# A three-block model on one core: weight-stream buffers paired into the experts' ring, three expert tiles moved ahead in the load order

## The chip, the core and the metric

The kernel runs on one core of one Trainium2 chip. The metric is the time of one execution on the device, in microseconds (us), as a median over runs. The core has five engines that matter here: TensorE (PE, matmuls; PEld is its weight load), VectorE (DVE), ScalarE (ACT), GpSimd (POOL) and SyncE (SP), which here does hardly anything but issue loads. Sixteen DMA engines move the data of all queues.

## The reference, cut to what matters

Three transformer-like blocks run one after another on 256 tokens of width 1024, all in fp32. The first has two layers (a state-space mixer, then attention, each with a SwiGLU feed-forward network, FFN, of width 2816). The second has a mixer (RWKV-7 and stick-breaking attention) whose output goes through the output weights w_out_2 (1024 x 1024), and a mixture of 32 experts, of which each token takes 4:

```python
top_logit, top_idx = lax.top_k(logits, TOP_K)
hid = xb @ w1[e] + b1[e]                    # 1024 -> 2048
glu = jnp.minimum(hid[:, :D_FF_EXPERT], SWIGLU_LIMIT)
lin = jnp.clip(hid[:, D_FF_EXPERT:], -SWIGLU_LIMIT, SWIGLU_LIMIT)
act = glu * jax.nn.sigmoid(SWIGLU_ALPHA * glu) * (lin + 1.0)
return (act @ w2[e] + b2[e]) * gate[:, None]  # 1024 -> 1024
```

One expert has 8 MB of w1 and 4 MB of w2; all 32 together have some 400 MB, read once. The third block is attention of two kinds and an output projection.

## The kernel before, in words

**Weights come through two readers.** Class `Stream` brings the weights of the blocks; class `Experts` brings those of the experts. Both issue their loads on SP's queue, in program order, and a load that must wait for its buffer holds up all SP loads behind it.

**The stream.** `weight_plan` writes the order of the loads by hand; `pieces` cuts each entry into pieces of at most 8 KB per partition (1 MB), most entries into two. The pool "w" has eight buffers of 8 KB per partition. `Stream.load` (L286) issues the next piece while there is room; a new piece takes the buffer that was given back first, whichever piece had it. `_split` (L299) turns one unit of a piece (two units to a piece, as a rule) into a high part on ScalarE (`wh`, L309) and a low part on VectorE or GpSimd (`wl`, L313); after the last unit of a piece `_retire` (L277) gives its buffer back. `ahead` keeps the splits three units ahead of the matmuls (two in the mixer), into four buffers (three in the mixer). `dense_F` takes three matmuls per product from these parts (helper line L514) and calls a background step (`tick`) after each unit. In the two FFNs the plan puts pieces named `ada_t` between the gate and up weights; `cond` (L1219, its operation L1225) reduces each with two VectorE operations in background steps and only then gives the buffer back.

**The second block's mixer** ends with `dense_F("w_out_2", ...)` (L1505): the first four of eight units multiply the attention half, the second four the output of `group_norm` (L1815), which runs in the background beside the first four and must be drained before the fifth. The 4 MB of w_out_2 are loaded in four pieces, as soon as w_in_2 frees buffers.

**The experts.** `moe` (L1905) opens a pool "ring" of nine buffers of 16 KB per partition, in the memory that the stream, the x pool and the mixer had (places 0 to 3 where the stream's 64 KB were, 4 and 5 over the x pool, 5 to 8 over the mixer's buffers), and loads as many of the 192 tiles of 2 MB as the ring takes, in the order of places in `RING`. A load waits for the last user of its place. An expert takes four tiles of w1 (`first`, L1994; 16 matmuls each) and two of w2 (`second`, L2043; 16 matmuls each); the order is w1 of expert 0, then w1 of e+1 and w2 of e in turn. `take` gives the tile before back and loads the next into its place. Ahead of the first expert the routing is computed, the largest count is read into registers, and `tc.If(n > 64)` (L1986 and L1987) branches over code for overfull experts, on every engine. With these inputs that code is jumped over.

After the experts the third block makes a new `Stream` with eight buffers.

Of the kernel before, what the change touches and what calls it, by code (L numbers as in the profile page):

```python
# [22 lines left out]
F32 = mybir.dt.float32  # L23
# [27 lines left out]
_n = 0  # L51
# [6 lines left out]
_n = 0  # L58
# [81 lines left out]

RING = [0, 1, 6, 7, 8, 2, 3, 5, 4]


EXPERTS = [(1, 0)] + [x for e in range(31) for x in ((1, e + 1), (2, e))] + [(2, 31)]
# [3 lines left out]
def weight_plan(stages):  # L150

    P = []
    G = []
    if "mod" in stages:
        P0 = [("ada_p", 0, 8, c * 512, 512, False) for c in range(4)]
        G = [("ada_t", r * 512, 4, 0, 1024, False) for r in range(14)]

    def fill(n):
        if "mod" in stages:
            P.extend(P0.pop(0) for _ in range(n))  # L160

    def mods(n):
        for _ in range(n):
            if G:
                P.append(G.pop(0))

    def cols(name, c0, n, nk=8, r0=0):
        P.append((name, r0, nk, c0, n, True))

    def rows4(name, total_k, ncol=1024, extra=iter(())):  # L170
        k = 0
        while k < total_k:
            n = min(4, total_k - k)
            P.append((name, k * 128, n, 0, ncol, True))
            mods(next(extra, 0))
            k += n

    def ffn(i):
        fill(2)
        at = iter(MODS[i])  # L180
        for q in range(6):
            n = 512 if q < 5 else 256
            for name in ("gate", "up"):
                cols(f"w_ffn_{name}{i}", q * 512, n)
                mods(next(at))
        rows4(f"w_ffn_down{i}", NQ, extra=at)
        P.append((f"w_ple{i}", 0, 2, 0, 1024, False))
        cols(f"w_ple_gate{i}", 0, 512)
        cols(f"w_ple_gate{i}", 512, 512)

    if "ssd" in stages:
        cols("w_in_mix", 2560, 16)
        for k, n in ((0, 2), (2, 2), (4, 4)):
            cols("w_in_mix", 2048, 512, n, k * 128)
        for c0 in (1024, 1536, 0, 512):
            cols("w_in_mix", c0, 512)
        for h in range(2):
            for b in (3600, 4624, 2576):
                cols("w_in_mix", b + 512 * h, 512)
        P.append(("w_out_mix", 1024, 4, 0, 1024, True))  # L200
        P.append(("w_out_mix", 1536, 4, 0, 1024, True))
        P.append(("w_out_mix", 0, 4, 0, 1024, True))
        P.append(("w_out_mix", 512, 4, 0, 1024, True))
        ffn(0)
    if "att" in stages:
        for c0 in (1024, 0, 512):
            cols("w_qkv", c0, 512)
        rows4("w_o", 8)
        ffn(1)
    assert not G  # L210
    if "mix" in stages:
        P.append("end")
        cols("w_in_2", 1536, 256)
        P.append(("lora", 0, 1, 0, 1024, False))
        for c0 in (512, 0, 1024, 1792, 2304, 2816):
            cols("w_in_2", c0, 512)
        P.append("end")
        rows4("w_out_2", 8)
        P.append("end")
    if "third" in stages:  # L220
        cols("w_in_3", 928, 512)
        cols("w_in_3", 1440, 512)
        cols("w_in_3", 0, 416)
        P.append(("w_uq", 0, 2, 0, 768, False))
        P.append(("w_ukv", 0, 1, 0, 1024, False))
        for c0 in (2464, 1952, 416, 4000, 4512, 2976, 3488):
            cols("w_in_3", c0, 512)
        P.append(("w_o_moba", 0, 4, 0, 1024, True))
        P.append(("w_o_mla", 0, 4, 0, 1024, True))
        cols("w_out_3", 0, 512)  # L230
        cols("w_out_3", 512, 512)
    return [c for e in P for c in ([e] if e == "end" else pieces(*e))]


def places():

    at, n = {}, 0
    for e in weight_plan(ALL):
        if e != "end" and e not in at:
            at[e] = n  # L240
            n += 128 * e[2] * e[4]
    return at


def pieces(name, r0, nk, c0, n, split):

    h = min(nk, 2048 // n)
    return [(name, r0 + k * 128, min(h, nk - k), c0, n, split) for k in range(0, nk, h)]


class Stream:


    def __init__(self, kb, plan, ring=8):
        self.kb, self.ring = kb, ring
        self.plan = []
        self.units = []
        self.fence = []
        unit = 1024
        for e in plan:  # L260
            if e == "end":
                self.fence.append(len(self.units))
                continue
            i = len(self.plan)
            self.plan.append(e)
            name, r0, nk, c0, n, split = e
            h = nk if not split else max(1, unit // n)
            for k in range(0, nk, h):
                self.units.append((i, k, min(h, nk - k), k + h >= nk, split))
        self.raws = {}  # L270
        self.splits = {}
        self.nsplit = self.used = 0
        self.pending = None
        self.room, self.nload = ring, 0
        self.depth = 3

    def _retire(self, i):  # L277
        self.room += 1
        self.load()

    def finish(self):
# [4 lines left out]
    def load(self):  # L286

        kb = self.kb
        while self.room and self.nload < len(self.plan):
            i = self.nload  # L290
            self.nload += 1
            self.room -= 1
            name, _, nk, _, n, split = self.plan[i]
            t = kb.wpool.tile([128, nk, n], F32, name=f"w_{name}_{i}", tag="w")
            o = kb.places[self.plan[i]]
            kb.nc.sync.dma_start(t.rearrange("p k n -> p (k n)"), kb.A["tiles"][o:o + 128 * nk * n].rearrange("(p m) -> p m", p=128))
            self.raws[i] = t
# [53 lines left out]
        return self.raws[i], lambda: self._retire(i)  # L351


class Experts:


    def __init__(self, kb, pool):
        self.kb, self.pool = kb, pool
        self.plan = [("exp_w1", e * 4 + k) if i == 1 else ("exp_w2", e * 2 + k) for i, e in EXPERTS for k in range(4 if i == 1 else 2)]
        self.buffers = [self.buffer(i) for i in range(len(RING))]  # L360
        self.free = list(RING)
        self.tiles, self.nload, self.used = {}, 0, 0

    def buffer(self, i):
        self._n = getattr(self, "_n", 0) + 1
        return self.pool.tile([128, 4096], F32, name=f"expert_{self._n}", tag=f"e{i}")

    def load(self):
        while self.free and self.nload < len(self.plan):
            i = self.free.pop(0)  # L370
            t, self.buffers[i] = self.buffers[i] or self.buffer(i), None
            name, r = self.plan[self.nload]
            src = self.kb.A[name][r * 128:r * 128 + 128]
            parts = 4 if self.nload == len(self.plan) - 1 else 1
            for c in range(0, 4096, 4096 // parts):
                self.kb.nc.sync.dma_start(t[:, c:c + 4096 // parts], src[:, c:c + 4096 // parts])
            self.tiles[self.nload] = i, t
            self.nload += 1
# [10 lines left out]
class KB:  # L389
# [2083 lines left out]
    def run(self):  # L2473
        nc, tc = self.nc, self.tc
        with ExitStack() as es:
            self.cpool = es.enter_context(self.pool("const", 1))
            self.fpool = es.enter_context(self.pool("residual", 1))
            outer = es
            es = outer.enter_context(ExitStack())
            self.wpool = es.enter_context(self.pool("w", 8))  # L2480
            self.xpool = es.enter_context(self.pool("x", 1))
            hes = ExitStack()
            self.hpool = hes.enter_context(self.pool("wsplit", 4))
# [7 lines left out]
                return _tl(pool, shape, dt, tag, bufs)  # L2491

            self.tl = tl
            self.st = Stream(self, weight_plan([n for n in self.stages if n != "third"]))
            xf = self.tl(self.fpool, [128, 8, T], F32, "xf")
            for k in (0, 4):
                nc.sync.dma_start(xf[:, k:k + 4], self.A["xT"][k * 128:k * 128 + 512].rearrange("(k p) n -> p k n", p=128))
# [30 lines left out]
            if "moe" in self.stages:  # L2528
                xf, stat = self.moe(xf, stat)
                self.dbg("xe", xf)  # L2530
            es = outer.enter_context(ExitStack())
            if "third" in self.stages:
                if "moe" not in self.stages:
                    with self.pool("ropetmp", 1) as C:
                        self.rope_tables(C)

                self.xpool = es.enter_context(self.pool("x", 1))
                self.wpool = es.enter_context(self.pool("w", 8))
                tpool = es.enter_context(self.pool("third", 1))
                self.st = Stream(self, weight_plan(["third"]))  # L2540
                self.st.load()
                self.third(xf, stat, tpool)
            else:
                nc.sync.dma_start(self.out.rearrange("(k p) n -> p k n", p=128), xf)
# [17 lines left out]
```

## Time and profile before

| | |
|---|---|
| median of 3 runs | 2274.73 us (2270.26 to 2278.99) |
| the profiled execution | 2268.43 us, its span 2266.6 us |
| PE, PEld busy | 94%, 66% of the span |
| DVE, ACT, POOL busy | 47%, 32%, 12% |
| moved by DMA | 618 MB, 273 GB/s on the mean |

A profile is one execution. Times in it count from the span's start. "Busy" is a share of the span; matmuls are pipelined, so that a PE in flight all the time need not be at its limit. In a row, `[4.37 <-PEq L1987]` means that the engine was idle for 4.37 us ahead of it, and what ended that. L514 is the helper that records nearly all matmuls; tiles tell them apart (acc<-expert,xe is the first expert product, py<-expert,aT the second).

### The profile page before, as it was taken

To read this page: it belongs to the slowest core of one execution; us is meant where nothing else is said; L and a number is where in the kernel's file an instruction comes from. 1 tells how busy PE (TensorE), PEld (TensorE's weight loads), DVE (VectorE), ACT (ScalarE), POOL (GpSimd) and SP (SyncE) were. 2 spreads that over 40 slices of the span, in tenths; PEclk is the share of its full clock that TensorE was granted. 3 is DMA by queue.
4 is the path that set the end of the run, shared out by engine and by line. 5 is a ranking of instruction groups with operands and counts; after the bars stand their busy time and mean duration, and the time that the engine had idled before them with its cause. 6 is when DMAs were issued, how large, how long until landed. Compare 5 with 4: busy or idle time off the path is not lost. (4 is left out here: it accounts for less than half of the span.)

```text
span 2266.6 us, 31625 instructions
## 1 busy us (share of the span) xinstructions
PE 2134.0 (94%) x13242; PEld 1500.3 (66%) x13242; DVE 1069.2 (47%) x2016; ACT 724.3 (32%) x1169; POOL 262.0 (12%) x141
## 2 busy tenths in 40 slices
PE   7999999999999988898899999999999999999997
PEld 7998998886998887788344444334333333368886
DVE  6775676566677667845122222322211212145665
ACT  5434543554544453343011110111111111133552
POOL 2332232000232002310000000000000000003101
PEclk9999999999999989898899999999999999999999
DMA  8434767432777531004999999999999999984320
GB/s 312 149 118 178 276 263 286 158 148 111 264 286 297 191 130 57 1 1 170 395 428 427 428 422 428 428 428 428 427 427 428 427 428 427 429 335 157 123 75 19
DMA packets 62098, 618.04 MB, mean 273 GB/s; under 512 B 7648, under 2 KB 10720, under 8 KB 12672
## 3 DMA queue, kind: packets, MB, share of 16 engines
q1 hardware_dynamic: 58768, 612.33, 66.8%
q10 hardware_dynamic: 3184, 3.65, 0.5%
q8 instruction: 106, 1.74, 0.3%
q14 instruction: 40, 0.33, 0.0%
HBM read 614.90 MB, written 1.05 MB: 272 GB/s over the span
## 5 line engine op out<-in xcount | busy, mean ns | idle before, releaser
L514 PE MATMUL acc<-xh,wh 128*128 128x256 f32 (+1 forms) x1736 | 494.5, 289 | 18.0 <-ACT wh L309 14.8
L514 PE MATMUL acc<-xl,wh 128*128 128x256 f32 (+1 forms) x1736 | 488.2, 285 | 1.1 <-DVE xl L553 0.3
L514 PE MATMUL acc<-expert,xe 128*64 128x512 f32 x2048 | 460.8, 600 | 28.0 <-DMA expert<-exp_w 23.5
L514 PE MATMUL acc<-xh,wl 128*128 128x256 f32 (+2 forms) x1704 | 483.4, 284 | 3.3 <-DVE wl L313 3.3
L514 PEld LDWEIGHTS acc<-expert,xe 128*64 128x64 f32 x2048 | 145.2, 138 | 313.2 <-issue 289.2
L514 PEld LDWEIGHTS acc<-xh,wh 128*128 128x128 f32 (+1 forms) x1736 | 328.2, 190 | 26.3 <-ACT wh L309 15.0
L514 PEld LDWEIGHTS acc<-xl,wh 128*128 128x128 f32 (+1 forms) x1736 | 329.5, 191 | 4.7 <-issue 1.4
L514 PEld LDWEIGHTS acc<-xh,wl 128*128 128x128 f32 (+2 forms) x1704 | 324.3, 190 | 5.6 <-DVE wl L313 4.7
L514 PE MATMUL py<-expert,aT 128*64 128x512 f32 x1024 | 234.4, 599 | 4.7 <-DMA expert<-exp_w 3.9
L2013 ACT ACTIVATE s<-a 128x512 f32<-128x512 f32 x32 | 20.2, 630 | 547.5 <-DVE a L2012 547.5
L2012 DVE TENSOR_SCALAR a<-acc 128x512 f32<-128x512 f32 x32 | 22.1, 691 | 360.3 <-PE acc L514 336.7
L2073 DVE SCALAR_TENSOR_TENSOR xf<-py,mod,xf 128x256 f32<-128x256 f32 x128 | 55.6, 479 | 283.9 <-PE py L514 283.9
L514 PEld LDWEIGHTS py<-expert,aT 128*64 128x64 f32 x1024 | 72.3, 138 | 138.3 <-issue 126.2
L313 POOL TENSOR_TENSOR wl<-w_w_in,wh 128x1024 fp32r<-128x1024 f32 (+1 forms) x11 | 26.7, 2428 | 1069.5 <-ACT wh L309 1049.6
L1225 DVE SCALAR_TENSOR_TENSOR w_ada_t<-w_ada_t,pe 128x1024 f32<-128x1024 f32 x56 | 93.3, 1688 | 0.0
L313 DVE TENSOR_TENSOR wl<-w_w_in,wh 128x1024 fp32r<-128x1024 f32 (+1 forms) x55 | 68.2, 1248 | 38.7 <-ACT wh L309 38.5
L309 ACT ACTIVATE wh<-w_w_in 128x1024 fp32r<-128x1024 f32 (+1 forms) x66 | 68.2, 1044 | 35.2 <-PE acc L514 35.1
L2060 ACT ACTIVATE y<-py 64x512 f32<-64x512 f32 x64 | 37.8, 591 | 119.2 <-PE py L514 118.6
L514 PE MATMUL tp<-sel,xh 128*128 128x128 f32 x512 | 64.3, 287 | 7.9 <-ACT aT L2040 6.9
L514 PE MATMUL acc<-wh,hh 128*128 128x512 f32 x176 | 68.7, 390 | 0.0
L514 PE MATMUL acc<-wh,hl 128*128 128x512 f32 x176 | 68.5, 389 | 0.0
L514 PE MATMUL acc<-wl,hh 128*128 128x512 f32 x176 | 68.5, 389 | 0.0
(657 smaller groups left out, 3307.9 us busy)
## 6 DMA issues: line engine op xcount, KB each, us to landing
expert<-exp_w SPq DMA_DIRECT2D x191, 2048.0 KB, 36.6
w_w_in<-tiles SPq DMA_DIRECT2D x31, 1024.0 KB, 4.9
w_ada_t<-tiles SPq DMA_DIRECT2D x28, 1024.0 KB, 6.4
w_w_ffn_gate<-tiles SPq DMA_DIRECT2D x22, 1024.0 KB, 5.0
w_w_ffn_up<-tiles SPq DMA_DIRECT2D x22, 1024.0 KB, 6.5
w_w_ffn_down<-tiles SPq DMA_DIRECT2D x22, 1024.0 KB, 6.4
w_w_in_mix<-tiles SPq DMA_DIRECT2D x21, 1024.0 KB, 8.6
w_w_out_mix<-tiles SPq DMA_DIRECT2D x8, 1024.0 KB, 4.8
```

The source lines that it names most:

```text
L309: kb.nc.scalar.activation(hi, w, AF.Copy)
L313: (kb.nc.gpsimd if far else kb.nc.vector).tensor_sub(lo, w, hi.bitcast(F32))
L514: self.nc.tensor.matmul(out, lhsT, rhs, start=start, stop=True, skip_group_check=True)
L1225: self.nc.vector.scalar_tensor_tensor(w[:, j], w[:, j], 1.0, crow[:, int(m >= 48)], op0=OP.mult, op1=OP.mult, accum_out=dst)
L2012: nc.vector.tensor_scalar(a, pg, 7.0, None, op0=OP.min)
L2013: nc.scalar.activation(s, a, AF.Sigmoid, scale=1.702)
L2060: nc.scalar.activation(y[r, o], py[r], AF.Copy)
L2073: nc.vector.scalar_tensor_tensor(xf[:, k], ps[o][:, c], gate2(k), xf[:, k], op0=OP.mult, op1=OP.add)
```

## The change

- The plan puts three entries ("early", k) between the two halves of w_out_2.
- The first `Stream` works in pairs: four buffers of 16 KB per partition (tags w0 to w3), each holding two pieces. Pairs are taken in the fixed order 3, 2, 1, 0; a new pair is begun only when both pieces that were in it are given back. The third block's stream stays as it was.
- An early entry takes a whole pair and loads an expert tile into it; that pair is never given back to the stream. The second half of w_out_2 thus comes into the pair of the first half.
- The pool "w" is opened first and stays open to the end of `moe`; its four pairs are places 0 to 3 of the ring, and the pool "ring" has places 4 to 8 alone. The three early tiles lie in places 2, 1 and 0. `RING`, the order of the other first loads, becomes 8, 7, 6, 3, 5, 4.

```diff
-RING = [0, 1, 6, 7, 8, 2, 3, 5, 4]
+RING = [8, 7, 6, 3, 5, 4]
+EARLY = 3
...
-        rows4("w_out_2", 8)
+        rows4("w_out_2", 4)
+        P.extend(("early", k) for k in range(EARLY))
+        P.append(("w_out_2", 512, 4, 0, 1024, True))
...
+    def buffer(self, p):
+        self._n = getattr(self, "_n", 0) + 1
+        return self.kb.wpool.tile([128, 4096], F32, name=f"w{p}_{self._n}", tag=f"w{p}")
+
     def _retire(self, i):
         self.room += 1
+        if self.busy:
+            self.busy[self.pair[i]] -= 1
         self.load()
...
         while self.room and self.nload < len(self.plan):
             i = self.nload
+            if self.busy:
+                early = self.plan[i][0] == "early"
+                if early and self.half % 2:
+                    self.half += 1
+                p = 3 - self.half // 2 % 4
+                if self.half % 2 == 0:
+                    if self.busy[p]:
+                        return
+                    t = self.fresh.pop(p, None)
+                    self.both = self.buffer(p) if t is None else t
+                self.busy[p] += 1
+                self.pair[i] = p
+                if early:
+                    name, r = experts_plan()[self.plan[i][1]]
+                    kb.nc.sync.dma_start(self.both, kb.A[name][r * 128:r * 128 + 128])
+                    self.early.append((p, self.both))
+                    self.half += 2
+                    self.nload += 1
+                    continue
+                self.half += 1
             self.nload += 1
             self.room -= 1
             name, _, nk, _, n, split = self.plan[i]
-            t = kb.wpool.tile([128, nk, n], F32, name=f"w_{name}_{i}", tag="w")
+            if self.busy:
+                o = (self.half - 1) % 2 * 2048
+                t = self.both[:, o:o + nk * n].rearrange("p (k n) -> p k n", n=n)
+            else:
+                t = kb.wpool.tile([128, nk, n], F32, name=f"w_{name}_{i}", tag="w")
...
-        self.buffers = [self.buffer(i) for i in range(len(RING))]
+        self.buffers = {i: self.buffer(i) for i in range(4, 9)}
         self.free = list(RING)
-        self.tiles, self.nload, self.used = {}, 0, 0
+        self.tiles = dict(enumerate(kb.st.early))
+        self.nload, self.used = len(self.tiles), 0
...
-            self.wpool = es.enter_context(self.pool("w", 8))
+            wes = outer.enter_context(ExitStack())
+            self.wpool = wes.enter_context(self.pool("w", 1))
...
-            self.st = Stream(self, weight_plan([n for n in self.stages if n != "third"]))
+            self.st = Stream(self, weight_plan([n for n in self.stages if n != "third"]), pairs=True)
...
                 xf, stat = self.moe(xf, stat)
                 self.dbg("xe", xf)
+            wes.close()
```

## Rows read from the trace of the kernel before

**Rows 1.** The page, part 2: GB/s in 40 equal slices of the span (56.7 us each).

```profile
GB/s 312 149 118 178 276 263 286 158 148 111 264 286 297 191 130 57 1 1 170 395 428 427 428 422 428 428 428 428 427 427 428 427 428 427 429 335 157 123 75 19
```

**Rows 2.** Stretches: length, busy time (instructions) of each engine, PEclk, DMA share, GB/s.

```profile
900.00:1040.00 140.00, 125.27 (x896) 110.25 (x895) 89.20 (x220) 51.31 (x90) 32.24 (x17) 0.94 0.01 2
...
1120.00:1400.00 280.00, 275.73 (x1340) 113.35 (x1337) 60.59 (x135) 34.61 (x66) 0.00 (x0) 0.99 1.01 427
```

**Rows 3.** Timeline of SP around the first expert loads: start, duration, what.

```profile
1052.79 1.28 SPq L376 DMA_DIRECT2D expert<-exp_w  x3
...
1060.77 0.33 SPq L376 DMA_DIRECT2D expert<-exp_w  x1
...
1101.59 0.34 SPq L376 DMA_DIRECT2D expert<-exp_w  x1
```

**Rows 4.** Instructions of L1987, the branch: ns min/median/max, first and last start.

```profile
L1987 SPq EVENT_SEMAPHORE  x8: 17/17/17, 1100.9 to 1101.5; - x8
...
L1987 PEldq COMPARE_BRANCH  x1: 6573/6573/6573, 1073.6 to 1073.6; - x1
```

**Rows 5.** Waits from 1060 to 1110: who for whom, total us, times, longest.

```profile
DVE a L2012 <- SPq L1987: 23.6, 1, 23.6
```

**Rows 6.** Timeline of PE over the first experts, merged.

```profile
1080.53 16.29 PE L514 MATMUL acc<-expert,xe 128*64 128x512 f32 x64 [4.37 <-PEq L1987]
...
1104.60 1.29 PE L2030 MATMUL tp<-ident,sg 128*128 128x128 f32 x4 [6.07 <-DVE sg L2025]
1105.82 15.60 PE L514 MATMUL acc<-expert,xe 128*64 128x512 f32 x64
...
1132.15 3.65 PE L514 MATMUL py<-expert,aT 128*64 128x512 f32 x16
1135.63 13.90 PE L514 MATMUL acc<-expert,xe 128*64 128x512 f32 x64
...
1190.20 13.90 PE L514 MATMUL acc<-expert,xe 128*64 128x512 f32 x64
```

**Rows 7.** Waits of PE from 1600 to 2010: total us, times, longest.

```profile
PE acc L514 <- DMA expert<-exp_w: 21.1, 21, 1.2
PE py L514 <- DMA expert<-exp_w: 3.9, 9, 0.8
```

**Rows 8.** Issue to landing: expert (1050 to 1085), w_out_2, ada_t.

```profile
DMA to landing us min/median/max: 7.9/26.5/40.1
...
DMA to landing us min/median/max: 4.8/4.8/4.8
...
DMA to landing us min/median/max: 4.7/6.4/9.1
```

**Rows 9.** Around w_out_2: SP, ACT and DVE timelines; w_in_2's last splits.

```profile
861.02 6.57 SPq L296 DMA_DIRECT2D w_w_out<-tiles  x2
...
L313 DVE TENSOR_TENSOR wl<-w_w_in,wh x11: 1210/1216/2909, 858.1 to 902.3; 128x1024 fp32r<-128x1024 f32 x11
...
1035.77 1.06 ACT L309 ACTIVATE wh<-w_w_out 128x1024 fp32r<-128x1024 f32 x1 [0.45 <-ACT wh L309]
...
1035.36 2.57 DVE L313 TENSOR_TENSOR wl<-w_w_out,wh 128x1024 fp32r<-128x1024 f32 x1 [1.65 <-ACT wh L309]
...
1040.34 0.69 DVE L1561 COPY f<-r8y 128x1024 f32<-128x1024 f32 x1
...
1042.45 0.42 DVE L1832 TENSOR_TENSOR b<-b,tp 128x256 f32<-128x256 f32 x1 [0.28 <-PE tp L1568]
```

**Rows 10.** Timelines of SP, ACT and DVE at one FFN gate of layer one.

```profile
254.57 0.33 SPq L296 DMA_DIRECT2D w_w_ffn_gate<-tiles  x1
...
272.06 1.07 ACT L309 ACTIVATE wh<-w_w_ffn_gate 128x1024 fp32r<-128x1024 f32 x1 [1.17 <-PE acc L514]
...
277.79 1.06 ACT L309 ACTIVATE wh<-w_w_ffn_gate 128x1024 fp32r<-128x1024 f32 x1 [1.83 <-PE acc L514]
...
271.35 1.21 DVE L1225 SCALAR_TENSOR_TENSOR w_ada_t<-w_ada_t,pe 128x1024 f32<-128x1024 f32 x1
```

More of the change, by code (lines that the diff above doesn't have):

```diff
@@ L231, in weight_plan @@
         cols("w_out_3", 512, 512)
-    return [c for e in P for c in ([e] if e == "end" else pieces(*e))]
+    return [c for e in P for c in ([e] if e == "end" or e[0] == "early" else pieces(*e))]
 def places():
@@ L238, in places @@
     for e in weight_plan(ALL):
-        if e != "end" and e not in at:
+        if e != "end" and e[0] != "early" and e not in at:
             at[e] = n
@@ L251, with __init__ @@
 class Stream:
-    def __init__(self, kb, plan, ring=8):
+    def __init__(self, kb, plan, ring=8, pairs=False):
         self.kb, self.ring = kb, ring
+        self.busy, self.half, self.pair, self.early = ([0] * 4 if pairs else None), 0, {}, []
+        self.fresh = {p: self.buffer(p) for p in range(4)} if pairs else {}
         self.plan = []
@@ L265, in __init__ @@
             self.plan.append(e)
+            if e[0] == "early":
+                continue
             name, r0, nk, c0, n, split = e
@@ L290, in load @@
             i = self.nload
+            if self.busy:
[16 more added lines that the diff above has]
+                    self.nload += 1
+                    continue
+                self.half += 1
             self.nload += 1
@@ L351, in hold, with experts_plan @@
         return self.raws[i], lambda: self._retire(i)
+def experts_plan():
+    return [("exp_w1", e * 4 + k) if i == 1 else ("exp_w2", e * 2 + k) for i, e in EXPERTS for k in range(4 if i == 1 else 2)]
 class Experts:
@@ L358, in __init__ @@
         self.kb, self.pool = kb, pool
-        self.plan = [("exp_w1", e * 4 + k) if i == 1 else ("exp_w2", e * 2 + k) for i, e in EXPERTS for k in range(4 if i == 1 else 2)]
-        self.buffers = [self.buffer(i) for i in range(len(RING))]
+        self.plan = experts_plan()
+        self.buffers = {i: self.buffer(i) for i in range(4, 9)}
         self.free = list(RING)
-        self.tiles, self.nload, self.used = {}, 0, 0
+        self.tiles = dict(enumerate(kb.st.early))
+        self.nload, self.used = len(self.tiles), 0
     def buffer(self, i):
         self._n = getattr(self, "_n", 0) + 1
-        return self.pool.tile([128, 4096], F32, name=f"expert_{self._n}", tag=f"e{i}")
+        pool, tag = (self.kb.wpool, "w") if i < 4 else (self.pool, "e")
+        return pool.tile([128, 4096], F32, name=f"expert_{self._n}", tag=f"{tag}{i}")
     def load(self):
@@ L370, in load @@
             i = self.free.pop(0)
-            t, self.buffers[i] = self.buffers[i] or self.buffer(i), None
+            t = self.buffers.pop(i, None)
+            t = self.buffer(i) if t is None else t
             name, r = self.plan[self.nload]
```

## The prediction

> **What bounds the kernel now.** I read the page's traffic first, then stretches around the expert stage, SP's own issue times, the matmul order, the waits, and last the places where the stream's buffers change hands. The traffic row [rows 1] shows slices 19 to 34 at about 427 GB/s. The stretches [rows 2] put the core's DMA share at 1.01 from 1120 us on, and at 0.01 from 900 to 1040: the stage that loads the experts is bound by DMA, and the 140 us ahead of it leave DMA unused. That PE looks full there too (275.73 of 280 us) does not make it the bound: two experts, 12 tiles, take 1190.20 - 1135.63 = 54.57 us of matmul order [rows 6], while DMA needs 12 x 4.9 = 58.8 us (2 MB at 427 GB/s). PE lives on the nine-tile backlog until about 1600 and then waits for tiles, 21.1 + 3.9 = 25.0 us in all [rows 7]. So an earlier end of DMA is worth its full amount up to about 25 us.
>
> The opening of the stage is where DMA loses time. SP issues the first tiles at 1052.79, the ninth at 1060.77, the tenth only at 1101.59 [rows 3]. Between them SP sits in the `If` of L1986/L1987: its eight semaphore instructions start at 1100.9 [rows 4], and the ninth load, issued at 1060.77, lands 40.1 us later [rows 8], at 1100.9. So SP leaves the `If` when all nine loads have landed, though tile 0 had been used up long before. VectorE waits for the same thing: a L2012 for 23.6 us [rows 5], of which PE feels only the end, inside the 6.07 us ahead of 1104.60 [rows 6]. With nothing queued the tenth load needs 7.9 us to land (the shortest in rows 8): 1109.5. From there DMA does not stop: 182 more loads x 4.9 = 891.8 us, last landing about 2001.
>
> **The three early tiles.** Three 2 MB loads move from 1052.79 into the idle stretch. Each waits on a pair: the first on the pair whose buffers serve the last w_out_2 loads today, 861 to 868 [rows 9], the others on the last w_in_2 splits, which start up to 902.3 [rows 9]. They cost three issues of 0.33 us on SP, which has nothing else to do there. With six tiles left, the ones in places 8, 7 and 6 of the ring are free once the group norm's last buffer there is read (f L1561, 1040.34 + 0.69 = 1041.0 [rows 9]); place 3 needs the last split, 5 and 4 the last matmuls. Six loads of 4.9 us from about 1045 land by about 1075, before the branch is reached or soon after. So SP's stall is gone.
>
> But the ring is then full and DMA idles until PE gives back tile 0. PE's first run is 16.29 us for four tiles; three at 13.90/4 = 3.47 leave 5.9 for the first [rows 6], so tile 0 is free at 1086.4, and the tenth load lands at 1086.4 + 0.1 + 7.9 = 1094.4: 15.1 us earlier than now. The 14th load needs tile 4: 1105.82 less some 2.6 us (PE was done at 1104.60 - 6.07 = 1098.5, VectorE was let go between 1100.9 and 1101.5), plus 15.60 - 3 x 3.47 = 5.2, is 1108.4, landing at 1116.4 against 1094.4 + 4 x 4.9 = 1114.0, so 2.4 lost; the 19th needs tile 9 (1132.15 + 3.65 - 2.6) and loses some 0.3. After that PE frees 12 tiles per 54.57 us, faster than DMA fills them. **Gain here: 15.1 - 2.7 = 12.4 us**, less every us by which PE starts later than 1080.53. It is not 3 x 4.9 because of the nine tiles, and it comes from the waiting `If` as much as from the early bytes.
>
> **The second half of w_out_2.** Three of four pairs now hold expert tiles, so this half can only be loaded into the pair of the first half, after its last split. That is the VectorE subtraction 1035.36 + 2.57 = 1037.9 [rows 9]; landing 4.8 us later [rows 8] is 1042.8. Today ScalarE starts the fifth unit's split at 1035.77, at once. Behind it wait, in order: on VectorE that unit's subtraction (1.2), then the group norm's multiplications, which begin at 1042.45 today. They would begin at 1042.8 + 1.1 + 0.1 + 1.2 = 1045.2, and PE's second half needs their result. **Cost 2.7 us**; bounds 0 (if VectorE's chain has that slack) and 5.1 (if the two loads share DMA and the first lands only with the second, 2.4 later). I take the worked value, since rows 8 has this very load. The fourth piece, landing 2.4 after, is split later still and costs nothing.
>
> **PE's branch.** PE's own jump at L1987 takes 6.573 us [rows 4], and PE is idle for 4.37 of it [rows 6]. It falls where expert loads have DMA full. After the change DMA has drained by then. The trace holds no jump of PE on an idle DMA, so the gain is between nothing and 4.37; I take 2.0, the middle, neither end being nearer. The Trainium skill ("Runtime: NRT & Kernel Launch", Instruction fetch mechanics) says that a taken branch outside the fetched pages must first fetch its page by DMA; no run here yet shows whether an idle DMA shortens it. By that rule the 2.0 would be nearer to 4.37 and the sum 2 us better.
>
> **The pairs.** Before, each load takes whichever of eight buffers came free first: 254.57 for a gate piece, when an older gate piece was split [rows 10]. After, pairs go round in fixed order, and in the two FFNs a pair of gate pieces follows, four pairs later, on a pair of ada_t pieces that VectorE holds for long. The gate load then waits for the last ada_t operation: 271.35 + 1.21 = 272.6, 18 us later than today. It lands at 277.4, where its first split starts at 272.06 today. PE needs that unit three units on: the split two units later starts at 277.79, one unit of PE is (277.79 - 272.06)/2 = 2.9, so 280.7. Split after landing: 277.4 + 1.06 + 0.1 + 1.21 = 279.8. **It is hidden, but by 0.9 us only.** The cover is the depth of three split units. Worked for all eight such places (four per FFN, the same rhythm), the margins are 0.35 to 1.7 us. ScalarE and VectorE stand still for 5 us each time and must catch up. I take 2 us for all eight; bounds 0 (every margin holds) and 11.5 (each load lands as late as a second one in its pair, 2.4 more, and the margins are overrun). If landing is 6.4 us, as the median of ada_t in rows 8, the cost is 5. The lora piece holds its pair as well, but the loads behind it serve splits that run on to 902.3, and today SP has issued this whole stream by 868 [rows 9]: taken as hidden. Startup, attention and the third block keep their order: DMA is far from full there [rows 1], and the third's first loads wait for the last expert tiles either way. Costed at nothing, covered by lead times of some 5 us and more beyond landing.
>
> **Sum.** 12.4 - 2.7 + 2.0 - 2.0 = 9.7 us. The profiled execution took 2268.4, so 2258.7 by it. The median of the runs shown is 6.3 higher; against 2274.7 it is **2265 us**, 0.43% less. A difference of 0.5%, 11.4 us, is about what a measurement of this kernel can tell from no change.
>
> **Rivals.**
> (a) PE's branch gives back nearly all its 4.37 us and the FFN cost is nil: 2274.7 - (12.4 - 2.7 + 4 - 0) = about 2261. For it: DMA is drained at the branch; margins are positive in all eight places. Against: a fetch has a cost of its own. Chance 0.3. The Trainium skill's rule of the branch (the section named above) points to this side.
> (b) The pairs stall PE: at the eight gate places the first split comes later than PE needs it. With landings of 7.2 us instead of 4.8 the cost is 11.5 instead of 2 and the time 2274.5, no gain. It decides for slower when the overrun exceeds about 1.4 us per place, that is a landing 2.4 us later than I assume; if ScalarE's and VectorE's standstill also delays the next ada_t release, each place drags the next and 16 to 25 us are lost: about 2285. For it: margins under 1 us in six of eight places. Against: the load is the first of its burst, on an empty queue. Chance of no gain 0.12, of slower 0.1.
> (c) The early tiles bring nothing that lasts: the ring is full anyway, PE is the real pace and DMA only follows. Then the gain is only the 2.6 us of VectorE's wait and the branch, less 2.7 and 2: about 2275. Against: PE's 25 us of waits after 1600. Chance 0.08.
> The forecast has 0.4.
>
> **How the numbers follow.** The likeliest case spans 2260 to 2270 (branch 0 to 4.37, w_out_2 0 to 5.1). To leave no more than 2 in 10 out, the range takes in (a) and the no-gain cases: 2257 to 2277. Faster by over 0.5% (under 2263.4): (a) and a quarter of the forecast, 0.4. Slower by over 0.5%: the bad end of (b), 0.1. Within: 0.5.
>
> **What would show it.** Right: three expert issues between about 867 and 910; two w_out_2 issues near 1038; ring place 8 issued near 1041; SP's L1987 instructions near 1080 rather than at 1100.9; an idle DMA of some 10 us just ahead of the first give-back; the last expert landing some 10 us before 2001; PE's waits for tiles starting later than 1600 minus the gain in backlog and totalling some 10 to 15 us. For the pairs: gate loads issued at the end of the ada_t operation, and PE without new waits on wh or wl in 250 to 400 and 600 to 740. Wrong: PE waits there; DMA gaps recurring after 1140; w_out_2's second half landing after 1045; PE starting on the experts after 1084.

## The result: 18 us slower, and the profile after

The changed kernel took 2290.67 us (median of five runs, 2287.33 to 2292.87) against 2272.84 for the kernel before on the same chip: a ratio of 1.0073, 95% interval 1.0061 to 1.0086. The forecast was 2265, its range 2257 to 2277. The profiled execution has a span of 2289.3 us against 2266.6. The ratios in this document are estimated from all runs beside each other, so they are not quite the quotients of the medians; and the two profiled executions lie 22.7 us apart, the medians 17.8, so the steps below add up to the larger figure.

To see where the time went, each ScalarE instruction of the new trace was set beside the same instruction of the old one. How much later it starts, along the kernel before's time:

| at (kernel before, us) | what starts there | later by (us) |
|---|---|---|
| 250 | first feed-forward stage (FFN) | 0.5 |
| 432 | after it | 14.9 |
| 554 | second FFN | 16.2 |
| 800 | after it | 34.3 |
| 1044 | end of the second block's output weights | 40.5 |
| 1106 | first experts, after the branch | 31.8 |
| 1300 | experts | 31.6 |
| 1888 | late experts | 21.8 |
| 2211 | third block | 21.5 |

So the experts' part did gain, 40.5 - 21.8 = 18.7 us, more than forecast. It was lost before it began: the two FFNs cost 14.4 + 18.1 = 32.5 us where 2 had been written down.

The stretches of the first FFN, from after its first gate piece on, show the loss. First the kernel before (length, busy time and instructions of PE, PEld, DVE, ACT and POOL, granted clock, DMA share, GB/s):

```profile
255.00:375.00 120.00, 120.00 (x972) 118.00 (x972) 85.85 (x91) 54.48 (x62) 31.72 (x12) 1.00 0.70 266
```

The same work after the change:

```profile
255.00:390.00 135.00, 125.98 (x977) 122.10 (x976) 90.63 (x92) 53.23 (x62) 32.29 (x12) 0.97 0.58 236
```

TensorE had not one idle microsecond there, 120.00 of 120.00 at clock 1.00. Now the same matmuls stretch over 135: 9.0 idle and 6.0 more counted as busy. The granted clock was at half (1.2 of 2.4 GHz) twice in this stretch, for 3.4 us from 335.0 and from 376.0, behind 3.4 and 3.0 us of idle time; that accounts for at most 3.4 of the 6.0, and the rest is not resolved here. In the second FFN, 150 us became 167 (first the kernel before):

```profile
585.00:735.00 150.00, 150.00 (x1121) 143.59 (x1120) 110.87 (x118) 67.47 (x74) 39.46 (x16) 1.00 0.74 278
...
602.00:769.00 167.00, 158.03 (x1124) 148.40 (x1123) 115.58 (x118) 64.02 (x72) 37.90 (x15) 0.98 0.57 232
```

Who waits there (after the change, 250 to 400 and 580 to 800; total, times, longest):

```profile
ACT wh L349 <- DMA w<-tiles: 38.8, 8, 11.7
...
ACT wh L349 <- DMA w<-tiles: 54.7, 12, 11.7
```

The kernel before has no wait of a weight's split for its load at either place. What SyncE waits for in 250 to 400, after the change:

```profile
SPq L336 <- DVE w L1272: 130.1, 6, 24.7
```

L1272 is VectorE's operation on the ada_t tiles. The loads come in bursts right behind it. SyncE's loads after the change, one line for each burst (start, time from there to the end of the last issue):

```profile
273.16 3.13 SPq L336 DMA_DIRECT2D w<-tiles  x6
...
297.24 3.02 SPq L336 DMA_DIRECT2D w<-tiles  x6
...
325.11 3.00 SPq L336 DMA_DIRECT2D w<-tiles  x6
...
351.04 2.08 SPq L336 DMA_DIRECT2D w<-tiles  x4
...
375.32 0.80 SPq L336 DMA_DIRECT2D w<-tiles  x2
```

and ScalarE's first split behind each of the first three:

```profile
278.13 2.01 ACT L349 ACTIVATE wh<-w 128x1024 fp32r<-128x1024 f32 x2 [6.70 <-DMA w<-tiles]
...
302.09 2.02 ACT L349 ACTIVATE wh<-w 128x1024 fp32r<-128x1024 f32 x2 [7.92 <-DMA w<-tiles]
...
330.08 2.00 ACT L349 ACTIVATE wh<-w 128x1024 fp32r<-128x1024 f32 x2 [11.75 <-DMA w<-tiles]
```

Each time the split begins 4.9 to 5.0 us after the issue: the transfer itself is about as short as in [rows 8]. The wait grows from 6.70 to 11.75 because the issue comes later each time. Behind the fourth burst it is 7.93. These four waits are 34.3 of the 38.8 us; the other four, 4.5 in all, stand at the split behind, which waits for the burst's second piece.

Around the experts the picture is the forecast's. SyncE, answering to [rows 3, 9]:

```profile
902.51 36.45 SPq L321 DMA_DIRECT2D w<-exp_w  x3
1075.30 0.81 SPq L336 DMA_DIRECT2D w<-tiles  x2
1078.47 50.42 SPq L423 DMA_DIRECT2D expert<-exp_w  x9
```

The branch, answering to [rows 4]:

```profile
L2034 SPq EVENT_SEMAPHORE  x8: 17/17/17, 1113.2 to 1113.8; - x8
...
L2034 PEldq COMPARE_BRANCH  x1: 3893/3893/3893, 1113.8 to 1113.8; - x1
```

TensorE over the first experts, answering to [rows 6]:

```profile
1118.00 10.52 PE L561 MATMUL acc<-w,xe 128*64 128x512 f32 x48 [2.60 <-PEq L2034]
...
1136.56 1.12 PE L2077 MATMUL tp<-ident,sg 128*128 128x128 f32 x4 [2.89 <-DVE sg L2072]
```

SyncE leaves the branch 3 us after it came, not 30. TensorE's branch takes 3.893 us and not 6.573, a tile of the first run takes 10.52 x 16/48 = 3.5 us where the first one took 5.9, and the gap ahead of `sg` is 2.89 and not 6.07. TensorE's waits for expert tiles, 1622 to 2032, are 20.4 us, somewhat smaller than the 25.0 of [rows 7] but not the 10 to 15 of the forecast:

```profile
PE acc L561 <- DMA expert<-exp_w: 18.4, 17, 2.4
PE py L561 <- DMA expert<-exp_w: 2.0, 6, 0.6
```

### The profile page after: what moved, and what is told of

Its sections match the earlier page's. It is cut to its first block, busy times and chain, and to the rows that moved or that the text cites. A ratio compares the mean times of both kernels' runs of the same rounds, so it can differ in the third digit from the quotient of the medians.

```text
span 2289.3 us, 31597 instructions
## 1 busy us (share of the span) xinstructions
PE 2147.9 (94%) x13242; PEld 1512.7 (66%) x13242; DVE 1081.9 (47%) x2016; ACT 721.5 (32%) x1169; POOL 262.6 (11%) x141
## 5 line engine op out<-in xcount | busy, mean ns | idle before, releaser
L561 PE MATMUL acc<-expert,xe 128*64 128x512 f32 x2000 | 446.8, 597 | 18.5 <-DMA expert<-exp_w 18.4
L353 DVE TENSOR_TENSOR wl<-w,wh 128x1024 fp32r<-128x1024 f32 x205 | 283.7, 1393 | 194.9 <-ACT wh L349 194.3
L349 ACT ACTIVATE wh<-w 128x1024 fp32r<-128x1024 f32 (+1 forms) x263 | 271.7, 1054 | 253.1 <-PE acc L561 135.2
L561 PEld LDWEIGHTS acc<-xh,wl 128*128 128x128 f32 (+2 forms) x1704 | 326.6, 192 | 16.7 <-DVE wl L353 11.5
L561 PEld LDWEIGHTS acc<-expert,xe 128*64 128x64 f32 x2000 | 140.5, 137 | 294.6 <-issue 275.5
L353 POOL TENSOR_TENSOR wl<-w,wh 128x1024 fp32r<-128x1024 f32 (+1 forms) x58 | 147.2, 2539 | 561.2 <-ACT wh L349 520.1
L1272 DVE SCALAR_TENSOR_TENSOR w<-w,pe 128x1024 f32<-128x1024 f32 x56 | 86.7, 1571 | 0.0
```

The lines of the kernel that those rows point to most:

```text
L349: kb.nc.scalar.activation(hi, w, AF.Copy)
L353: (kb.nc.gpsimd if far else kb.nc.vector).tensor_sub(lo, w, hi.bitcast(F32))
L561: self.nc.tensor.matmul(out, lhsT, rhs, start=start, stop=True, skip_group_check=True)
L1272: self.nc.vector.scalar_tensor_tensor(w[:, j], w[:, j], 1.0, crow[:, int(m >= 48)], op0=OP.mult, op1=OP.mult, accum_out=dst)
```

## The experiments

Theory A was that the fixed order of the pairs made the FFNs lose; B, that it was the pairing, since a pair comes free only with its second piece. Four kernels ran together, with the kernel before at 2275.56 us beside them.

**Pairs in the order in which they come free.**

```diff
-                p = 3 - self.half // 2 % 4
                 if self.half % 2 == 0:
-                    if self.busy[p]:
+                    if not self.ready:
                         return
+                    self.last = self.ready.pop(0)
+                p = self.last
...
+            if not self.busy[p] and not (self.half % 2 and p == self.last):
+                self.ready.append(p)
```

> The changed kernel, except that a pair is taken in the order in which pairs come free, not always in the order 3, 2, 1, 0. Theory A (the two feed-forward stages lose 33 us because a fixed order makes a weight's load wait for a pair that still holds a slow ada_t tile, while another pair is already free): the 33 us vanish, the experts' 18.6 us stay, about 2257 us. Theory B (a pair comes free only when both its pieces have been split, which takes away a piece of lead whatever the order): the loss stays, about 2290 us. Theory C (the loss has nothing to do with buffers, but with where the code or the data lie): about 2290 us too.

Measured: 2256.76 us, ratio 0.9921 (0.9906 to 0.9936). The whole loss is gone; its shift against the kernel before stays between -0.6 and 1.0 us up to 860. The first FFN's stretch:

```profile
255.00:375.00 120.00, 120.00 (x972) 118.02 (x971) 85.87 (x91) 54.44 (x62) 31.80 (x12) 1.00 0.67 265
```

Pairs as such cost nothing, and theory C, that the loss has nothing to do with buffers, falls: only the choice of the pair differs. This version has the lowest median here, 0.8% under the kernel before and, by the two ratios, 1.5% under the changed one.

**Pairs in fixed order, no tile put between the halves.**

```diff
-RING = [8, 7, 6, 3, 5, 4]
-EARLY = 3
+RING = [1, 0, 8, 7, 6, 3, 2, 5, 4]
+EARLY = 0
```

> The changed kernel without the three expert tiles between the halves of w_out_2: all nine ring places are loaded from the experts' stage on, as before the change, and the stream keeps its four pairs in fixed order. Theories A and B: the loss of some 33 us in the two feed-forward stages stays and the gain at the branch and in the experts goes, about 2300 to 2306 us. If the early tiles themselves disturbed the stream (rival), the loss would shrink: under 2290 us.

Measured: 2293.22 us, ratio 1.0078 (1.0063 to 1.0094). The FFN loss is there in full (36.2 us later at 800, 2.0 of them from before the FFNs). The time lies between the expectation's two figures, but the edit did not do what the expectation says. Two expert tiles still went out early, at 922.5 and 939.9, since the pairs that stay in the ring had been free since the second block's input weights:

```profile
903.65 0.80 SPq L336 DMA_DIRECT2D w<-tiles  x2
922.54 207.55 SPq L423 DMA_DIRECT2D expert<-exp_w  x11
```

So it is the pairs staying in the ring that makes tiles early; what the three entries between the halves add is the third one.

**Eight single buffers in fixed order**, on the kernel before.

```diff
             i = self.nload
+            if self.fixed and i >= 8 and i - 8 not in self.gone:
+                return
...
-            t = kb.wpool.tile([128, nk, n], F32, name=f"w_{name}_{i}", tag="w")
+            t = kb.wpool.tile([128, nk, n], F32, name=f"w_{name}_{i}", tag=f"w{i % 8}" if self.fixed else "w")
```

> The kernel before, with its eight single buffers of 8 KB, except that piece i always goes to buffer i mod 8 and waits until that one's piece has been released; experts as before. Theory A (order): the loss appears without any pair, about 2300 us (2290 to 2306). Theory B (pairing): no loss, 2270 to 2276 us.

Measured: 2270.07 us, ratio 0.9980 (0.9968 to 0.9991). Theory A, as it stood, falls: the order alone costs nothing. Nor does pairing alone, by the first kernel. Only the two together do. SyncE's gate loads of this kernel at the same places (start; each line's first issue is the gate's first piece):

```profile
266.46 0.33 SPq L300 DMA_DIRECT2D w_w_ffn_gate<-tiles  x1
...
272.11 0.33 SPq L300 DMA_DIRECT2D w_w_ffn_gate<-tiles  x1
...
290.51 3.75 SPq L300 DMA_DIRECT2D w_w_ffn_gate<-tiles  x2
...
312.26 0.33 SPq L300 DMA_DIRECT2D w_w_ffn_gate<-tiles  x1
...
316.83 0.33 SPq L300 DMA_DIRECT2D w_w_ffn_gate<-tiles  x1
```

In the same fixed order a single buffer lets the gate's first piece go when the first ada_t piece is released, 266.46, and its second when the second one is, 272.11. A pair sends both at 273.16. The splits here wait for a load three times, 6.3 us in all, 2.4 the longest, and TensorE stays 120.00 of 120.00 busy:

```profile
ACT wh L313 <- DMA w_w_ffn_gate<-tiles: 6.3, 3, 2.4
```

The second pieces went at 272.11, 293.9 (290.51 + 3.75, less the 0.33 of one issue) and 316.83, the pairs of the changed kernel at 273.16, 297.24 and 325.11: 1.1, 3.3 and 8.3 us later, of which 1.1 is how far the two kernels were apart before the stage. At the fourth place the two issues, the pair's and its second piece's, are at 351.04 and 340.26: 10.8 us. That growth is the drag. Behind a late gate piece ScalarE and VectorE stand still, VectorE's next ada_t operations come later, and so does the next pair's release. How much of the loss is the drag and how much that six loads then go out at once was not separated by a run; the waits above (34.3 us for the first piece, which lands as fast as before, 4.5 for the second) speak for the late issue as the larger part.

**Pairs in first-free order, two early tiles**, so that w_out_2's second half has a pair of its own.

```diff
-RING = [8, 7, 6, 3, 5, 4]
-EARLY = 3
+RING = [8, 7, 6, 2, 5, 3, 4]
+EARLY = 2
```

(2 and 3 stand for the pairs of the first and second half.)

> Pairs in the order in which they come free, as in the first kernel, but two expert tiles early and not three, so that the second half of w_out_2 has a pair of its own and needn't wait for the first half's release; the ring then has seven places loaded afterwards, five of them before the branch. Theory A: the FFNs' loss is gone and w_out_2's 2 to 3 us with it, while two tiles of lead give some 4 to 5 us less than three: 2254 to 2262 us. Theory B: about 2290 us.

Measured: 2261.40 us, ratio 0.9945 (0.9931 to 0.9958). The FFNs lose nothing here either. TensorE's branch is 6.05 us again:

```profile
L2041 PEldq COMPARE_BRANCH  x1: 6053/6053/6053, 1076.2 to 1076.2; - x1
```

This raised the second question: does TensorE's branch take longer beside transfers (theory D) or not (E)? Four more kernels ran together, the kernel before at 2271.01 us.

**Four tiles ahead of the branch**, on the kernel before.

```diff
-        self.free = list(RING)
+        self.free = list(RING[:4])
...
             self.free.append(self.tiles.pop(self.used - 1)[0])
+            if self.used == 1:
+                self.free.extend(RING[4:])
```

> The kernel before, with only four of the nine ring places loaded ahead of the branch; the other five join the ring when the first expert tile is given back. Theory D (TensorE's branch is slow because the tile transfers run beside it): the four tiles land by about 1074 us, the branch takes 3.4 to 4 us in place of 6.57 and TensorE starts on the experts 3 to 4 us earlier; some 10 us without transfers are then paid back in the part from 1340 us on, where the experts wait for their tiles, so the whole is 2276 to 2284 us. Theory E (the branch takes what it takes, the transfers have no part in it): 6.5 us again, no earlier start, and the whole is 2280 to 2288 us.

Measured: 2280.36 us, ratio 1.0040 (1.0027 to 1.0054), within D's range and at the edge of E's. The branch tells them apart:

```profile
L1989 PEldq COMPARE_BRANCH  x1: 4013/4013/4013, 1074.8 to 1074.8; - x1
```

4.0 us, by a change of the transfers alone. The traces also show what goes on within the branch. The row of one kind of transfer in the kernel before, over its branch, 1073.6 to 1080.4 (packets, MB, share of 16 engines):

```profile
q8 instruction: 1, 0.02, 1.0%
```

In all ten kernels of this document the last such packet to land within the branch, 16 KB of instructions, takes 0.9 to 1.3 us, and the branch ends 1.4 us after it. Where transfers were ending or over when the branch came, this packet begins 1.1 to 1.6 us into the branch; where they ran on, 3.4 to 4.6. So what differs is how late this packet begins; that it is the branch's own is read from the constant 1.4 us.

The kernel with four tiles ahead loses in all: from 1044 to 1106 it gains 8.4 us, and from there to 1888 it gives back 12.8.

**Six tiles ahead of the branch, three right behind it**, on the kernel before.

```diff
-        ex.load()
+        ex.load(6)
...
             self.moe_overflow(xf, hT, gd, pos)
+        ex.load()
```

> The kernel before, with six ring places loaded ahead of the branch and three right behind it. SyncE's wait at the branch falls from 30.5 us to about 15, so that the tenth tile's load follows the first give-back (about 1085 us) and not 1101.6 us, while transfers run on beside TensorE's branch. If that wait costs what the idle transfer slots of the kernel before show (4.4 us, by 46 and 143 of 428 units short in two slices of 10 us), the part from 1340 us on gains 3 to 5 us and the start of the experts nothing: 2268 to 2272 us. If the wait is covered by the nine tiles already there: no change, 2275 us.

Measured: 2274.00 us, ratio 1.0013 (1.0000 to 1.0026): no change that can be told. The expectation had it the wrong way round. The opening gained 4.2 us (VectorE is no longer held by SyncE's wait, the gap ahead of `sg` is 2.89):

```profile
1100.50 0.94 PE L2031 MATMUL tp<-ident,sg 128*128 128x128 f32 x4 [2.89 <-DVE sg L2026]
```

and the later part gave 3.8 of it back, because no byte had moved earlier.

**Two early tiles, the ninth place held back until the first give-back.**

```diff
-RING = [8, 7, 6, 2, 5, 3, 4]
+RING = [8, 7, 6, 2, 5, 3]
...
             self.free.append(self.tiles.pop(self.used - 1)[0])
+            if self.used == 1:
+                self.free.append(4)
```

> The kernel with pairs in first-free order and two early tiles (2261.4 us), with the ninth place held back until the first give-back, so that the transfers are over when TensorE branches, as they were with three early tiles. Theory D: the branch takes 3.4 to 4 us in place of 6.05, the clock does not fall behind it, and 3 to 4 us come back: 2256 to 2259 us. Theory E: no change, 2261 us, or more.

Measured: 2259.93 us, ratio 0.9952 (0.9933 to 0.9971). Branch 3.793 us, as D says; the total lies between the two theories' figures and is too near to the 2261.40 of two early tiles, which ran beside other kernels, to be told from it.

**The same, with the two early tiles behind w_out_2's second half** (`EARLY = 0`, the two free pairs first in the ring).

> As the last kernel, but no tile is put between the halves of the second block's output weights: the two expert tiles follow the second half on SyncE and still start early, since their two pairs have been free since the second block's input weights. The wait for the second half (1.6 us with two early tiles between, 3.2 us with three) goes: 2254 to 2258 us. If that wait was the stage's own and not the order's: as the last kernel.

Measured: 2262.36 us, ratio 0.9945 (0.9925 to 0.9966). A miss that taught something. There is no wait for w_out_2 left, yet the shift still grows by 3.2 us there, from 2.4 to 5.6. Stretches of 4 us of this kernel:

```profile
1038.00:1042.00 4.00, 4.00 (x34) 4.00 (x32) 3.73 (x10) 1.06 (x1) 1.24 (x1) 0.87 0.00 0
1042.00:1046.00 4.00, 4.00 (x20) 4.00 (x20) 2.44 (x6) 0.00 (x0) 0.00 (x0) 0.50 0.40 86
```

and of the changed kernel, where ScalarE does wait 7.43 us for that load:

```profile
1074.00:1078.00 4.00, 4.00 (x28) 4.00 (x28) 3.59 (x14) 0.00 (x0) 0.19 (x1) 0.72 0.41 121
1078.00:1082.00 4.00, 4.00 (x20) 4.00 (x20) 1.20 (x2) 1.06 (x1) 0.00 (x0) 0.50 1.07 453
```

In both TensorE is busy without a break, at half its clock (1.2 of 2.4 GHz). The kernel with the ninth place held back has 1.00 there and no step at all (1.95 before and behind):

```profile
1038.00:1042.00 4.00, 4.00 (x37) 4.00 (x38) 3.66 (x12) 0.78 (x1) 0.79 (x1) 1.00 0.00 0
```

## What sets the end of the experts' stage

The last column is how much later than in the kernel before the same late eviction starts (`y<-py`, 1887.79 us there). The sum beside it uses only transfers: when the ring's loads could begin against 1052.8, 4.9 us off for each tile loaded before, and the idle transfer time over the next slices of 10 us against the 4.4 us of the kernel before (10 x (1 - GB/s / 428) over the slices under 400 GB/s).

| kernel | begin | early tiles | slices under 400 GB/s | idle over 4.4 | sum | measured |
|---|---|---|---|---|---|---|
| changed | +27.2 | -14.7 | 52, 287, 362 | +9.2 | +21.7 | +21.8 |
| first free, three early | -8.9 | -14.7 | 220, 138, 359 | +8.9 | -14.7 | -14.9 |
| pairs, fixed, none put between | +28.7 | -9.8 | 324, 82, 362 | +7.6 | +26.5 | +26.5 |
| fixed singles (one early by itself) | +5.1 | -4.9 | 385, 283 | 0.0 | +0.2 | +0.1 |
| two early | -8.7 | -9.8 | 37, 388, 367 | +7.1 | -11.4 | -11.0 |
| four ahead | +1.5 | 0 | 244, 233 | +4.5 | +6.0 | +5.9 |
| six ahead | -0.3 | 0 | 252 | -0.3 | -0.6 | -0.7 |
| ninth held | -9.7 | -9.8 | 188, 218 | +6.1 | -13.4 | -13.5 |
| behind the halves | -9.3 | -9.8 | 201, 77 | +9.1 | -10.0 | -10.3 |

(For the two with three early tiles the ring's loads begin behind those of w_out_2's second half; the time taken is that at which the first of its two pieces has landed, 1080.0 and 1043.9.) Nine kernels within 0.5 us: the stage ends when its transfers do. This is bookkeeping, since the idle time is itself read from the traces; it shows where a gain counts, not how long the queue will stand idle. The branch, `sg` and the first run enter only where they delay the give-back that an idle queue waits for, as part of the idle time.

## Why the prediction was wrong, by its steps

- **The pairs: the step that failed.** Written down were 2 us, bounds 0 to 11.5; measured 32.5. The working for the first place was right almost to the microsecond: load at 272.6 (273.16), landing at 277.4 (278.0), no lasting loss (the shift is back at 0.54 us at 289). The failure was to multiply it: "worked for all eight such places ... the same rhythm" took each place's release from the trace of before. But the release is an operation on the engine that the late load holds up, so each place starts later than the one ahead of it. The cover was also worth less than it looked: TensorE was 120.00 of 120.00 busy, so what overruns the margin is lost whole, and behind the longest stalls the granted clock was at half, which took up to 3.4 of the 15 us in the first FFN.
- **Rival (b)** named this drag, at 16 to 25 us and a chance of 0.1, and 2285 us. Its first cause, landings of 7.2 us, didn't happen (4.9 to 5.0); its second, the standstill that delays the next release, did, and the FFNs lost 32.5, more than its 25. Being a recurrence, the drag should have been followed through the four places, not priced as a worst end.
- **The three early tiles and the branch: right in mechanism, 4 us too small.** Forecast 12.4 + 2.0 = 14.4; measured 18.7. The tenth load went at 1121.69 - 40.5 = 1081.2 of the kernel before's time, not 1086.5. TensorE started 2.7 us earlier than before, and the first tile took 3.5 and not the 5.9 taken from the kernel before, whose clock had been low. The early tiles went at 902.5, 921.7 and 938.6, less the shift of 35.2 at 867.3, 886.5 and 903.4, inside the 867 to 910 forecast.
- **PE's branch: 2.0 forecast, right, but by luck**, since it was the middle of an open range. It takes 2.7 us less, and TensorE's idle time at it falls from 4.37 to 2.60. The runs now show what had been open: 3.4 to 4.0 us in the five kernels whose transfers were ending or over when the branch came (3.393, 3.653, 3.793, 3.893, 4.013), 5.9 to 7.1 in the five where they ran on (5.913, 6.053, 6.173, 6.573, 7.111). The Trainium skill ("Runtime: NRT & Kernel Launch", Instruction fetch mechanics) says that a taken branch outside the fetched pages has to fetch its page by DMA; the ten branches agree with that. In the traces (above) it is the time until an instruction packet begins that grows.
- **w_out_2's second half: 2.7 forecast, 3.2 to 3.3 seen, but not shown to be that.** ScalarE waits, as forecast; TensorE does not, it works on at half clock. Two kernels without the wait, fixed singles and the last one, have the same 3.2 us at the same clock. In the changed kernel the two overlap, and which would have been seen alone stays open.
- **Rival (c)**, that early tiles bring nothing that lasts, is refuted by the table and by the first kernel, 14.9 us ahead of the kernel before at 1888: they are what lasts, and what the opening alone wins (six ahead) does not.
- Startup and attention, costed at nothing, add 0.5 and 1.3 us; mixer and what follows up to the output weights 3.0. The kernel with fixed singles, whose first expert tile goes at 1039.9, has a step of 2.2 us near 960 too, so they aren't put down to the early tiles.

## What to carry to other kernels

A ring that goes round in fixed order ties each load to the release of one particular older tile; with larger buffers it ties it to the last piece in that buffer. Before fixing an order, find the slowest tile to be released and the load that inherits its place; if that release itself waits for work behind the load, follow it through several rounds, since the delay grew from place to place here. In a stage that is bound by transfers, count when bytes start and when the queue stands idle: time won on the engines is given back unless it ends such an idle stretch sooner. And where the order can be first-free at no cost, as here, take that: the same early tiles were then worth 0.8%.

## What had not been expected of the hardware

The clock moved the total by several microseconds at places that no edit touched: 3.2 us at the end of the second block's output weights, with the granted clock at 0.50 or 1.00 over the same matmuls, busy all the while, in kernels that differ only in which tiles were loaded when. What the runs don't show is what decided it. With that, the versions in first-free order (2256.76, 2261.40, 2259.93 and 2262.36 us) can't all be ranked. All runs of the first (2250.40 to 2258.28) lie under those of the one with two early tiles beside it (2258.75 to 2265.34), but whether by the third tile or by such a place of the clock stays open; the table gives the third tile 3.9 us (-14.9 against -11.0).
